# A 1024 x 1024 output projection by seven half-size products instead of eight plain tiles, with the projection before it reordered by row pairs

## Chip, cores and metric

The kernel runs on one core of a Trainium2 chip. The metric is the time of one execution on the device in microseconds. TensorE (PE; its weight loads PEld) multiplies matrices into PSUM, VectorE (DVE), ScalarE (ACT) and GpSimd (POOL) do elementwise work, SyncE (SP) mostly issues DMAs; ACT and POOL issue some too.

## The reference

One layer of a hybrid streaming encoder over 512 prompt frames and 64 sample frames (576 columns in all), in float32:

```python
def layer(x, lp, st):
    h = x + 0.5 * swiglu(rmsnorm(x, lp['norm_ffn1']), lp['w_ffn1_in'], lp['w_ffn1_out'])
    mix, new_st = mixer(rmsnorm(h, lp['norm_mix']), lp, st)
    h = h + mix
    h = h + 0.5 * swiglu(rmsnorm(h, lp['norm_ffn2']), lp['w_ffn2_in'], lp['w_ffn2_out'])
    return h, new_st
```

The mixer has three branches (a state-space scan, banded attention, a matrix memory). What matters here is its end:

```python
    g_ssd, g_att, g_ml = jnp.split(jax.nn.sigmoid(gl), 3, axis=-1)
    merged = (g_ssd * (y_ssd @ lp['w_proj_ssd']) + g_att * (y_att @ lp['w_proj_attn'])
              + g_ml * (y_ml @ lp['w_proj_mlstm']))
    return merged @ lp['w_out'], (...)
```

`w_out` and `w_proj_ssd` are 1024 x 1024, the other two 512 x 1024. A final RMSNorm follows the layer.

## The kernel before

Activations lie transposed: 1024 channels as 8 rows (tiles of 128 partitions), 576 frames along the free axis. All matmuls take float32 operands cut in two (`split`, L339 to L342): a high piece, the value rounded to the matmul's format (ScalarE cast, L340), and a low piece, the rest (VectorE subtraction, L341). A product of two operands is three matmuls: high x high, high x low, low x high.

There are two ways of multiplying.

*Plain tiles* (`gemm`, L314). The weights of 128 output channels come by two SP loads of 128 x 512 into the ring `wr` (5 buffers) and are split into the rings `ph` and `pl` (6 each). One tile covers the 576 columns in two parts (HALVES, L35), 256 and 320 wide, each a group of 8 k-steps x 3 matmuls on L281 into one of six PSUM banks taken in turn (`bank`, L200, which begins at 0 in each `wide`), and a callback empties the bank. `half_major` takes the first parts of several tiles, then their second parts; `order` turns that round.

*Seven products* (`stream`, L609, and `product`, L740). A unit is a 1024 x 256 block of weights and two output rows; weights, data and outputs are cut in 2 x 2 blocks, with 288 (FH) columns to a half, and seven products of sums and differences of blocks replace eight. Each product is 4 k-steps x 3 matmuls, 128x288, on L747. The products are called X1, A11, X3, X4, A22, A21, X2 after their weight piece. `fetch_sums` (L563) loads two blocks of a unit's weights into `x12` (ring `wx`, 4 buffers) and adds two more with an accumulating DMA from GpSimd's queue, which gives the weights of X1 and X2; `fetch` loads three single blocks into `wr`; `operand` (L591) gives the piece for one product. In the feed-forwards (`self.mixer` false) X3's weights are made in place from X1's by a GpSimd addition, and X4's from X3's by another (L594 to L598). Pieces are prepared five products ahead (AHEAD). `residual` (L778) adds one product to the residual rows in `R1` by one VectorE instruction (L786): X1 and A11 complete the second half of the first row of a pair; X3, X4, A22, A21 belong to the second row; X2 completes the first half of the first row. X1, A22, X3 and X2 of a unit accumulate in one bank, X4 and A21 in another, A11 alone. `fetch_sums` issues its load on GpSimd's queue while `self.behind` is over 0, else on SP behind a weight load of the feed-forward (`loads_after`).

The order on each engine is not that of the text: the program is laid out by a simulated timeline, which keeps dependencies, and each engine then runs its queue in that order. `high_priority` moves work ahead in it, and `issue_after(i)` places what is issued within it, on the engine of `i`, behind `i`.

The parts of the program: first feed-forward ("a", plain tiles, then a stream that ends with the four output units of its last quarter), mixer, `merge` (L1541), second feed-forward ("c": `norm`, eight plain tiles of which the first three are half-major, meanwhile the moving pieces of its stream, then the stream).

In `merge`, `half(1, ..)` and `half(2, ..)` project attention and matrix memory; the callback `put` gates a finished half tile (VectorE, L1581) and adds it into `merged` (GpSimd, L1583). The gates come from DRAM in the order of `gates` (L1557), five ahead; `self.last` is the last of these loads. Then the eight tiles of `w_proj_ssd` follow in order of rows, the last three half-major (L1626 to L1633). The residual rows are loaded back from `xs` into `R1` on GpSimd's queue behind `self.last`. Each half row of `merged` is split into `XH` and `XL`, and the eight plain tiles of `w_out` run, three half-major, two in turn, three half-major; `res` adds each half tile to `R1` (L1643). Only then `run` sets `self.behind` to 4 (L1692), so that the second feed-forward's first four `x12` loads go by GpSimd's queue, behind `self.last`.

## Time and profile before

| what | us |
|---|---|
| median of 3 runs | 1893.77 |
| lowest, highest | 1893.25, 1894.69 |
| the profiled execution | 1896.08 |
| its span, first to last instruction | 1894.4 |
| first matmul of `w_out` | 1274.44 |
| first matmul of the tile after it | 1326.53 |

The mean granted TensorE clock was 0.995 of full speed. The page gives each engine's busy time and, in 40 slices of 47 us, the tenths of a slice in which it was busy. A row of a group gives its line, engine, operation, `out<-in`, shape, count, then busy us, mean ns of one, and the engine's idle time just before, with what ended it. A row of stretches gives start:end, length, busy us and number of instructions of PE, PEld, DVE, ACT and POOL, the granted clock, the DMA share and GB/s; an instruction that crosses an edge is counted on both sides. A row of the timeline gives start, duration, engine, line, operation, and in brackets the idle time before it. A row of waits names who waited, for whom, us in total, times, and the longest. Matmuls overlap: their spacing from start to start is what counts, not their duration.

### The profile page before, as it was taken

Reading aid. Unit: us, or ns where it says so; the run is one execution under the profiler, and the core shown is the slowest. Engines: PE = TensorE matmul, PEld = TensorE weight load, DVE = VectorE, ACT = ScalarE, POOL = GpSimd, SP = SyncE. Lnnn points to the kernel's source line nnn. Section 1 sums busy time; section 2 is a strip of 40 time slices with the busy share of each in tenths; the row PEclk is TensorE's granted clock in tenths of the full one; section 3 lists DMA queues with packets and bytes.
Section 4 is the critical chain, followed back from the end, with each engine's and each line's share of the span. In section 5 each row is a group of like instructions: output and inputs, shape, how many; then the busy total and the mean of one; then the engine's idle time right before and its main releaser. Section 6 shows DMA issues by size and latency. Waiting matters only on the chain. (4 is left out here: it accounts for less than half of the span.)

```text
span 1894.4 us, 37651 instructions
## 1 busy us (share of the span) xinstructions
PE 1853.9 (98%) x13863; PEld 1807.0 (95%) x13863; DVE 1555.9 (82%) x2768; ACT 1080.1 (57%) x2438; POOL 701.4 (37%) x659
## 2 busy tenths in 40 slices
PE   9899999999999999999999999999999999999998
PEld 9899999999999879889999999999999999999998
DVE  7998998988998867767778777745899998999864
ACT  6554554655555677677666676334465554554544
POOL 3443343334231324523635453630343334333311
PEclk9999999999999999999999999999999999999999
DMA  7456556566575465755656655742446656666521
GB/s 221 110 154 167 162 153 173 157 179 173 153 203 162 116 175 159 216 156 134 188 157 185 175 163 178 238 142 77 119 118 175 165 157 164 166 163 165 152 100 57
DMA packets 130896, 299.62 MB, mean 158 GB/s; under 512 B 14464, under 2 KB 26368, under 8 KB 130712
## 3 DMA queue, kind: packets, MB, share of 16 engines
q1 hardware_dynamic: 100248, 206.24, 32.3%
q0 software_dynamic: 20848, 76.29, 21.6%
q10 hardware_dynamic: 9616, 14.69, 2.5%
q8 instruction: 109, 1.79, 0.4%
q14 instruction: 75, 0.61, 0.1%
HBM read 276.90 MB, written 20.26 MB: 157 GB/s over the span
## 5 line engine op out<-in xcount | busy, mean ns | idle before, releaser
L747 PE MATMUL acc<-TH,ph 128*128 128x288 f32 x3332 | 996.5, 300 | 21.5 <-ACT uv L655 7.9
L747 PE MATMUL acc<-TL,ph 128*128 128x288 f32 x3332 | 989.0, 297 | 0.7 <-DVE TL L341 0.7
L747 PE MATMUL acc<-TH,pl 128*128 128x288 f32 x3332 | 982.1, 296 | 2.4 <-DVE pl L341 2.4
L747 PEld LDWEIGHTS acc<-TH,ph 128*128 128x128 f32 x3332 | 626.5, 188 | 36.2 <-ACT uv L655 9.9
L747 PEld LDWEIGHTS acc<-TH,pl 128*128 128x128 f32 x3332 | 629.0, 189 | 4.7 <-DVE pl L341 3.1
L747 PEld LDWEIGHTS acc<-TL,ph 128*128 128x128 f32 x3332 | 628.5, 189 | 4.6 <-issue 3.0
L341 DVE TENSOR_TENSOR pl<-wr,ph 128x512 fp32r<-128x512 f32 x467 | 453.8, 978 | 75.3 <-ACT ph L340 64.8
L340 ACT CAST ph<-wr 128x512 fp32r<-128x512 f32 x467 | 284.9, 617 | 241.4 <-PE acc L747 134.7
L341 DVE TENSOR_TENSOR pl<-wx,ph 128x512 fp32r<-128x512 f32 x406 | 330.2, 817 | 40.7 <-ACT ph L340 34.9
L340 ACT CAST ph<-wx 128x512 fp32r<-128x512 f32 x406 | 246.7, 619 | 200.1 <-POOL wx L594 122.9
L594 POOL TENSOR_TENSOR wx<-wx,wr 128x512 f32<-128x512 f32 x168 | 258.8, 1540 | 205.5 <-DVE pl L341 163.1
L582 POOL DMA_DIRECT2D wx<-in_sblk x119 | 104.9, 914 | 504.0 <-DVE pl L341 232.4
L281 PE MATMUL acc<-YH,ph 128*128 128x320 f32 (+1 forms) x640 | 188.5, 297 | 1.4 <-ACT ph L340 0.8
L281 PE MATMUL acc<-YL,ph 128*128 128x320 f32 (+1 forms) x640 | 189.0, 296 | 0.1
L281 PE MATMUL acc<-YH,pl 128*128 128x320 f32 (+1 forms) x640 | 188.5, 295 | 0.0
L281 PEld LDWEIGHTS acc<-YH,ph 128*128 128x128 f32 x640 | 120.3, 189 | 2.4 <-ACT ph L340 1.2
L281 PEld LDWEIGHTS acc<-YL,ph 128*128 128x128 f32 x640 | 120.8, 189 | 0.6 <-DVE YL L398 0.5
L281 PEld LDWEIGHTS acc<-YH,pl 128*128 128x128 f32 x640 | 120.7, 189 | 0.0
L594 POOL TENSOR_TENSOR wy<-wx,wr 128x512 f32<-128x512 f32 x35 | 63.2, 1805 | 113.7 <-DVE pl L341 101.8
L786 DVE SCALAR_TENSOR_TENSOR R<-acc,R 128x288 f32<-128x288 f32 x196 | 87.8, 450 | 16.3 <-PE acc L747 15.2
L340 ACT CAST TH<-g 128x288 fp32r<-128x288 f32 x140 | 59.6, 432 | 55.8 <-POOL g L772 31.5
L341 DVE TENSOR_TENSOR pl<-wy,ph 128x512 fp32r<-128x512 f32 x70 | 57.1, 822 | 26.6 <-ACT ph L340 25.7
(331 smaller groups left out, 2351.3 us busy)
## 6 DMA issues: line engine op xcount, KB each, us to landing
wr<-in_sblk SPq DMA_DIRECT2D x357, 256.0 KB, 3.6
wx<-in_sblk POOLq DMA_DIRECT2D x123, 512.0 KB, 6.4
wx<-in_sblk SPq DMA_DIRECT2D x115, 512.0 KB, 3.7
wr<-in_wblk SPq DMA_DIRECT2D x110, 256.0 KB, 3.0
R<-scr_rows ACTq DMA_DIRECT2D x12, 576.0 KB, 6.1
gs<-g SPq DMA_DIRECT2D x20, 288.0 KB, 4.3
g<-gs POOLq DMA_DIRECT2D x20, 288.0 KB, 4.5
y<-ys POOLq DMA_DIRECT2D x12, 288.0 KB, 5.9
```

What stands on the lines that cost most here:

```text
L281: last = nc.tensor.matmul(ps[:, :n], wt[:, wsl], xx[:, k0 + k, a:a + n], start=(k == 0 and i == 0), stop=(k == nk - 1 and i == 2))
L340: self.cast = self.nc.scalar.copy(hi, src).ins
L341: self.nc.vector.tensor_tensor(lo, src, hi.bitcast(F32), op=ALU.subtract)
L582: nc.gpsimd.dma_start(x12, src[:, 1:3, :], accum_op=ALU.add)
L594: add = lambda o, one, two: self.nc.gpsimd.tensor_tensor(o, one, two, op=ALU.add)
L747: self.nc.tensor.matmul(ps, wt[:, wsl], xx[:, kk, :], start=(start and kk == 0 and i == 0), stop=(kk == 3 and i == 2), skip_group_check=True)
L786: self.nc.vector.scalar_tensor_tensor(o, ps, scale, o, op0=ALU.mult, op1=ALU.add)
```

## The change

`w_out` becomes four units of seven products, in the same order of products and banks as the feed-forward's stream, with `residual` in place of `res`. For it:

- `w_proj_ssd`'s tiles (and their gates) run in the order of rows 0, 4, 1, 5, 2, 6, 3, 7, which completes the pair (k, k+4) of `merged` after each two tiles. The last two, rows 3 and 7, run half-major with the second halves first.
- `operands(k)` makes the moving pieces of one pair: five subtractions and seven splits of 288 columns; it stands behind each two tiles. X1 is b22, A11 b12 - b22, X3 b11 - b22, X4 b11, A22 b22 - b21, A21 b12 - b11, X2 b21 - b11, where the first index is the row of the pair and the second the half.
- The pieces lie in buffers of the merge that have been read: those of `YH` and `YL`, four of `y`, two of the gates' ring, four of `uv`, and two new tiles.
- The first weight loads of all four units are issued by GpSimd behind the last gate load (`self.held` keeps them for the stream), the accumulating loads behind an addition into `merged`.
- The additions of weights on GpSimd are queued behind the last addition into `merged` (`adds_after`).
- `self.behind` is set in `merge`, and not again after it.

```diff
-NB = 55
-NS = 119
+NB = 47
+NS = 123
...
+class Pairs(list):
+
+    def __getitem__(self, at):
+        p, k, t = at
+        return super().__getitem__(k // 2)[p, k % 2, t]
...
+        self.held, self.adds_after = deque(), None
...
+        if self.held:
+            return self.held.popleft()
         i = len(self.splan)
...
-        add = lambda o, one, two: self.nc.gpsimd.tensor_tensor(o, one, two, op=ALU.add)
+
+        def add(o, one, two):
+            with self.tc.issue_after(self.adds_after) if self.adds_after else nullcontext():
+                self.nc.gpsimd.tensor_tensor(o, one, two, op=ALU.add)
...
-        gates = deque((8 * b + n) for b in (1, 2, 0) for n in range(8))
+        turns = (0, 4, 1, 5, 2, 6, 3, 7)
+        gates = deque((8 * b + n) for b in (1, 2, 0) for n in (range(8) if b else turns))
...
-                    nc.gpsimd.tensor_tensor(merged[:, n, sl], merged[:, n, sl], t, op=ALU.add)
+                    self.added = nc.gpsimd.tensor_tensor(merged[:, n, sl], merged[:, n, sl], t, op=ALU.add).ins
...
-        tiles = [(("w_proj_ssd", 0, 1024, n * 128, 128), [(0, put(n, 0))]) for n in range(8)]
-        self.gemm(tiles[:4], ZH, ZL)
-
+        tiles = [(("w_proj_ssd", 0, 1024, n * 128, 128), [(0, put(n, 0))]) for n in turns]
+        self.gemm(tiles[:2], ZH, ZL)
+        two = iter([self.mp.tile([128, 2, FH], F32R, name=f"W{v}{i}", tag=f"{v}{i}", bufs=1)
+                    for v in "HL" for i in range(8)])
+        pair = lambda: Pairs((next(two), next(two)))
+        late, soon = [self.xp.tile([128, 4, FH], F32R, name=f"W{i}") for i in range(2)]
+        ys = [Pairs(self.mp.tile([128, 2, FH], F32R, name="W", tag="y", bufs=4) for _ in range(2)) for _ in range(2)]
+        ops = {self.T_X1: [soon, Pairs(self.gp.tile([128, 2, FH], F32R, name="W", tag="g", bufs=BUFS["g"]) for _ in range(2))],
+               self.T_A11: [pair(), Rows(self.gp.tile([128, FH], F32R, name="uv", tag="uv", bufs=4) for _ in range(4))],
+               self.T_X3: [pair(), pair()], self.T_X4: [pair(), pair()], self.T_A22: [pair(), pair()],
+               self.T_A21: [pair(), ys[0]], self.T_X2: [ys[1], late]}
+
+        def operands(kk):
+            b11, b12, b21, b22 = (merged[:, k, h * FH:(h + 1) * FH] for k in (kk, kk + 4) for h in range(2))
+            sub = lambda o, one, two: nc.vector.tensor_tensor(o, one, two, op=ALU.subtract)
+            put = lambda src, t: self.split(src, *(v[:, kk, :] for v in ops[t]))
+            put(b22, self.T_X1)
+            for t, b in ((self.T_A11, b12), (self.T_X3, b11)):
+                d = self.xp.tile([128, FH], F32, name="d", tag="d", bufs=2)
+                sub(d, b, b22)
+                put(d, t)
+            put(b11, self.T_X4)
+            for t, one, two in ((self.T_A22, b22, b21), (self.T_A21, b12, b11), (self.T_X2, b21, b11)):
+                sub(one, one, two)
+                put(one, t)
+
+        units = [("w_out", 0, 256 * m, 256 * m + 128) for m in range(4)]
+        operands(0)
+        self.gemm(tiles[2:4], ZH, ZL)
+        self.behind = WBUFS["wx"]
+        self.held.extend([self.fetch_sums(u) for u in units])
         with tc.issue_after(self.last):
             for k in range(0, 8, 2):
                 nc.gpsimd.dma_start(self.R1[:, k:k + 2, :], self.xs[:, k:k + 2, :])
+        operands(1)
         self.gemm(tiles[4:5], ZH, ZL)
-        self.gemm(tiles[5:], ZH, ZL, half_major=True)
-        XH, XL = rows()
...
-        tiles = [(("w_out", 0, 1024, n * 128, 128), [(0, res(n))]) for n in range(8)]
-        self.gemm(tiles[:3], XH, XL, half_major=True)
-        self.gemm(tiles[3:5], XH, XL)
-        self.gemm(tiles[5:], XH, XL, half_major=True)
+        self.sums_after = self.added
+        self.gemm(tiles[5:6], ZH, ZL)
+        operands(2)
+        self.gemm(tiles[6:], ZH, ZL, half_major=True, order=(1, 0))
+        operands(3)
+        self.mixer, self.adds_after = False, self.added
+        order = ((0, self.T_X1), (1, self.T_A22), (0, self.T_A11), (1, self.T_A21), (0, self.T_X3), (1, self.T_X2),
+                 (0, self.T_X4))
+        self.stream([(u, ops, self.residual(self.R1, m, None)) for m, u in enumerate(units)], order,
+                    lambda n: {self.T_X1: n % 3, self.T_A11: 3, self.T_X4: 4 + n % 2})
+        self.adds_after = None
...
-        self.behind = WBUFS["wx"]
```

More of the change, by code (lines that the diff above doesn't have):

```diff
@@ L1631, in merge @@
                 nc.gpsimd.dma_start(self.R1[:, k:k + 2, :], self.xs[:, k:k + 2, :])
+        operands(1)
         self.gemm(tiles[4:5], ZH, ZL)
-        self.gemm(tiles[5:], ZH, ZL, half_major=True)
-        XH, XL = rows()
-        for a, n in HALVES:
-            for k in range(8):
-                sl = slice(a, a + n)
-                self.split(merged[:, k, sl], XH[:, k, sl], XL[:, k, sl])
-        def res(n):
-            def go(h, ps, sl):
-                nc.vector.scalar_tensor_tensor(self.R1[:, n, sl], ps, 0.5, self.R1[:, n, sl], op0=ALU.mult, op1=ALU.add)
-            return go
-        tiles = [(("w_out", 0, 1024, n * 128, 128), [(0, res(n))]) for n in range(8)]
-        self.gemm(tiles[:3], XH, XL, half_major=True)
-        self.gemm(tiles[3:5], XH, XL)
-        self.gemm(tiles[5:], XH, XL, half_major=True)
+        self.sums_after = self.added
[9 more added lines that the diff above has]
+        self.adds_after = None
     def run(self):
```

## The prediction

> **What bounds the kernel now.** I read the page first (busy shares and slices), then the waits of TensorE around the merge, then the busy times of the stages.
>
> ```profile
> span 1894.4 us, 37651 instructions
> PE 1853.9 (98%) x13863; PEld 1807.0 (95%) x13863; DVE 1555.9 (82%) x2768; ACT 1080.1 (57%) x2438; POOL 701.4 (37%) x659
> ...
> PE   9899999999999999999999999999999999999998
> ...
> DVE  7998998988998867767778777745899998999864
> ```
>
> TensorE is busy for 98% of the span; the merge (1170 to 1326 us) is slices 26 to 28, counted from 1, where VectorE is at 7, 4 and 5 tenths and has room. The waits of TensorE from 1170 to 1400 us, the whole merge, the norm after it and the start of the second feed-forward, are one line:
>
> ```profile
> PE acc L281 <- ACT g L662: 0.5, 1, 0.5
> ```
>
> So matmuls alone set the end here: one removed is worth its own spacing, one that waits costs what it waits. Four stretches: the end of the last projection, `w_out` as it is, one that already runs in the form the change brings (the last four output units of the first feed-forward), and the one from the second feed-forward's norm to its stream:
>
> ```profile
> core 0: us, PE busy (x) PEld busy (x) DVE busy (x) ACT busy (x) POOL busy (x), PEclk, DMA share, GB/s
> 1260.00:1274.40 14.40, 14.40 (x106) 14.40 (x105) 7.00 (x14) 4.54 (x9) 4.16 (x4) 1.00 0.22 70
> 1274.40:1326.50 52.10, 52.10 (x394) 52.10 (x393) 31.02 (x63) 23.63 (x48) 1.95 (x2) 1.00 0.24 83
> 530.40:574.90 44.50, 44.50 (x336) 44.50 (x335) 42.55 (x76) 25.85 (x49) 13.48 (x12) 1.00 0.79 214
> 1335.20:1379.20 44.00, 44.00 (x326) 43.93 (x326) 41.40 (x75) 22.11 (x43) 20.57 (x14) 1.00 0.47 114
> ```
>
> The last projection leaves VectorE half its time free, `w_out` 21 us. The 28 products of the third row (530 to 575) fill TensorE for all of 44.5 us, with VectorE at 96%: no wait, but no room either. The last row has 2.6 us left on VectorE.
>
> **The change, part by part.**
>
> Products. Before: 8 tiles x 2 halves x 8 k x 3 = 384 matmuls, half 256 wide, half 320. After: 4 units x 7 products x 4 k x 3 = 336, all 288 wide.
>
> ```profile
> 1274.44 0.28 PE L281 MATMUL acc<-YH,ph 128*128 128x256 f32 x1
> 1274.56 0.28 PE L281 MATMUL acc<-YL,ph 128*128 128x256 f32 x1
> ...
> 1300.04 0.28 PE L281 MATMUL acc<-YH,ph 128*128 128x256 f32 x1
> ```
>
> First and last are the first matmuls of output tiles 0 and 4, so four tiles, 192 matmuls, take 25.60 us: 133.3 ns each (0.12 us between those of 256 columns). The 336 of the row from 530.4 take 44.5 us, 132.4 ns, and as windows count matmuls at both edges this is the same spacing. I take 133.3 for both: 48 fewer are **-6.4 us**. The last projection keeps its 384; its new order changes no count.
>
> Added work beside TensorE. Weight pieces: 28 of 128x512 instead of 16. Moving pieces: per row pair 7 splits and 5 subtractions of 288 columns, in all 28 and 20, instead of 16 splits. Residual additions: 28 instead of 16. GpSimd additions of weights: 8, where there were none.
>
> ```profile
> L341 DVE TENSOR_TENSOR pl<-wr,ph 128x512 fp32r<-128x512 f32 x17 | 12.3, 721 | 5.2 <-ACT ph L340 4.6
> ...
> L341 DVE TENSOR_TENSOR TL<-xk,TH 128x288 fp32r<-128x288 f32 x8 | 3.6, 448 | 0.0
> ...
> L340 ACT CAST TH<-g 128x288 fp32r<-128x288 f32 x140 | 59.6, 432 | 55.8 <-POOL g L772 31.5
> ...
> L340 ACT CAST ph<-wr 128x512 fp32r<-128x512 f32 x467 | 284.9, 617 | 241.4 <-PE acc L747 134.7
> ...
> L786 DVE SCALAR_TENSOR_TENSOR R<-acc,R 128x288 f32<-128x288 f32 x29 | 13.1, 450 | 1.3 <-PE acc L747 1.0
> ...
> L594 POOL TENSOR_TENSOR wx<-wx,wr 128x512 f32<-128x512 f32 x168 | 258.8, 1540 | 205.5 <-DVE pl L341 163.1
> ```
>
> VectorE gets 12 x 0.72 + (12 + 20) x 0.45 + 12 x 0.45 = 28 us more (16 old splits put at 0.45 too); ScalarE, at 45% here, 12 x 0.62 + 12 x 0.43 = 13 us by its casts of the same shapes. Three quarters of the moving pieces are made under the last projection's tiles, where VectorE has half its time free; `w_out` itself has the mix of the row from 530.4 and, like it, the next norm behind it. I cost this at **0** in steady state, hidden by matmuls as in 530 to 575; without that cover, the 28 us less the 21 free would show as 7.
>
> The start of `w_out`. Here the analogy ends: that stream was already running. The last two tiles (rows 3 and 7) run second half first, so X1 and A11, of second halves alone, are complete 2 x 24 x 0.12 = 5.8 us before the last tile ends. The third product, X3, needs a weight sum that may only be issued behind the last addition into `merged` (`adds_after`). The old chain of one first half:
>
> ```profile
> 1258.32 0.42 DVE L1581 SCALAR_TENSOR_TENSOR g<-g,acc 128x256 f32<-128x256 f32 x1
> ...
> 1258.82 0.74 POOL L1583 TENSOR_TENSOR merged<-merged,g 128x256 f32<-128x256 f32 x1 [1.45 <-DVE g L1581]
> ```
>
> Count from the gating's start, which is about the end of the last tile's matmuls. The addition is done at 0.50 + 0.74 = 1.24; the sum for X3 (1.54) at 2.8; its cast at 3.4, its low piece at 4.1. X1 and A11 occupy TensorE until -0.16 (a matmul's 0.28 less its spacing) + 2 x 1.6 = 3.0. X3 therefore waits 0.4 for the high piece and 0.4 for the low, and ends at 5.4. The sum for X4 overwrites the buffer that X3's split has read: 4.1 + 1.54, cast and split give 6.3 and 7.0: 1.3 more. In written order this is **2.1 us**. It is 0 if the order per engine, which the program lays out itself from a simulated timeline, puts unit 1's X1 and A11 (3.2 us) ahead of X3. The bounds: 0, as at the next stream's start (in the line of waits above), and 9.1, as at the first stream's start:
>
> ```profile
> 62.60:92.00 29.40, 24.20 (x152) 22.13 (x151) 27.57 (x54) 17.86 (x42) 12.81 (x7) 0.93 0.31 90
> ```
>
> 152 matmuls need 20.3 us of those 29.4. A gain is excluded: nothing waits there now. I take **+1.4**, nearer to the chain, the only one of the three with this kernel's new wait in it. Behind the weight sum on GpSimd stand only the later sums and, later, the norm's powers.
>
> GpSimd's additions slow VectorE:
>
> ```profile
> 536.82 1.59 POOL L594 TENSOR_TENSOR wx<-wx,wr 128x512 f32<-128x512 f32 x1
> ...
> 537.36 1.61 DVE L341 TENSOR_TENSOR pl<-wx,ph 128x512 fp32r<-128x512 f32 x1
> ```
>
> The split, 0.72 otherwise, ends only after the addition does. The Trainium skill, "SBUF — State Buffer", section "Who interferes with whom", has it that a VectorE instruction with two SBUF inputs contends with a GpSimd instruction that reads SBUF, the second to issue blocked outright; the row agrees, and the rule speaks against this change, which adds eight such additions to a stage that had none. By the rule alone (8 x 0.9 us of VectorE) the time is not changed further, as the six additions in 530 to 575 are in that row's 42.55 us.
>
> The end of `w_out`. The last product completes only row 6's first half; it and row 7 finish late, so the norm's sums are later. The same junction, first feed-forward to mixer:
>
> ```profile
> 574.91 0.29 PE L747 MATMUL acc<-TH,pl 128*128 128x288 f32 x1
> 575.04 0.28 PE L281 MATMUL acc<-XH,ph 128*128 128x256 f32 x1
> ...
> 588.81 0.97 PE L390 MATMUL ps_x<-ident,sm 128*128 128x128 f32 x6
> ```
>
> No matmul is late there. One thing differs: the last unit's accumulator is `n % 3`; there n was 43, bank 1, here it is 3, bank 0, the bank that the next `gemm` takes first. If its first tile isn't put behind another, it waits for the last residual: 0.16 + 0.45, or 1.3 with a split just ahead. Between 0 and 1.3 I take **+0.3**.
>
> The second feed-forward. Its norm factors come 588.81 - 575.04 = 13.8 us after its first matmul instead of these 8.0:
>
> ```profile
> 1326.53 0.28 PE L281 MATMUL acc<-YH,ph 128*128 128x256 f32 x1
> ...
> 1334.51 0.97 PE L390 MATMUL ps_x<-ident,sm 128*128 128x128 f32 x6
> ...
> 1370.93 0.45 DVE L341 TENSOR_TENSOR TL<-xk,TH 128x288 fp32r<-128x288 f32 x1
> ...
> 1379.20 0.29 PE L747 MATMUL acc<-TH,ph 128*128 128x288 f32 x1
> ```
>
> The last low piece of X1's data is ready 7.8 us before its stream begins; 5.8 of that go, less what VectorE's 2.6 us of idle time absorb. Bounds 0 and 1.5; **+0.2**. Its first four weight sums are now loaded by SP behind a tile's weights, as in the first feed-forward, instead of on GpSimd's queue; that is over 50 us before use, hidden by the eight plain tiles: 0. The four early loads and `xs` move on GpSimd's queue behind the last gate load, a few tiles ahead of use: 0. DMA is busy at 24% in `w_out` and at 79% in the analogue without a wait: 0.
>
> Sum: -6.4 + 1.4 + 0.3 + 0.2 = **-4.5 us**. The profiled execution took 1896.1 us (span 1894.4, 1.7 around it), 2.3 above the median of the runs; on it the sum gives 1891.6. On the median, 1893.8, it gives **1889.3**.
>
> **The rivals.**
>
> All of it (R1). The products whose pieces are ready go first and X3 comes late enough: -6.4 to -5.5, about 1887.8. For it: no wait at the next stream's start and none in the row from 530.4. Against it: two chained GpSimd sums begin only after the last tile.
>
> VectorE and GpSimd pace the start (R2). In the 13 us before and 8 after the last tile's end VectorE has two row pairs' pieces (2 x 12 x 0.45 = 10.8), 5 gatings, 6 weight splits and 4 residuals (8.4), and about 5 us of blocking by some ten GpSimd additions: 24 us of work in 21. If all shows, 1.4 becomes 4 to 5, and the time 1891 to 1893.5. For it: where the streams form pieces between products they lose time too:
>
> ```profile
> 484.00:508.00 24.00, 21.16 (x137) 19.67 (x136) 24.00 (x50) 10.75 (x24) 6.85 (x7) 0.93 0.62 169
> ```
>
> 137 matmuls need 18.3 of 24 us there, VectorE full. Against it: the last row pair's later pieces are due only at the sixth to eighth product.
>
> Slower (R3): the clock. One wait of TensorE is followed by half speed:
>
> ```profile
> 90.79 0.40 PE L747 MATMUL acc<-TH,ph 128*128 128x288 f32 x1 [1.93 <-ACT P L763]
> ...
> 91.20:94.60 3.40, 3.40 (x16) 3.40 (x16) 3.11 (x6) 1.58 (x5) 1.61 (x1) 0.51 0.55 172
> ```
>
> The granted clock is 0.51 for 3.4 us: some 12 matmuls, 1.6 us, lost on top of the 1.9. If X3 and X4 each come over 2 us late (from a weight sum that ends after 5 instead of 2.75), the start costs what the first stream's start did, 9.1 with its halved stretch, and with R2's remaining 2 us: -6.4 + 11.1 + 0.5, about 1899. For it: that row's VectorE was as full. Against it: there four row pairs' pieces were late, here one. The Trainium skill, "TensorE: Matmul & The Clock Gate", section "Why this matters for your kernels", allows gaps up to about 3 us before the clock falls; this trace disagrees with 1.9. By the page a 2 us wait would cost 2, by the trace 3.6.
>
> **How the numbers follow.** Forecast, 1888.4 to 1890.8: 0.45. R1, 1887 to 1888.4: 0.22. R2, 1890.8 to 1894: 0.25. R3: 0.08. A measurement here tells about 0.2%, 3.8 us, from no change. Faster by more (below 1890.0): R1 and 0.39 of the forecast, 0.61. Within: 0.06 of the forecast, R2 and 0.02 of R3, 0.33. Slower: 0.06. The range leaves out R3, the last of R2 and a tail below R1 less the runs' spread of 0.5: 1886.9 to 1893.5.
>
> **What would show it.** 336 matmuls of 288 columns on L747 in the merge at 133 ns, and no L281 with `w_out`: the 6.4. Waits of TensorE for `ph` or `pl` in the first 8 us: the 1.4; if for the moving pieces instead, R2. A granted clock under 1 there: R3. A gap at the first matmul of the next `gemm`, ended by a residual: the 0.3. Waits at the next stream's start: the 0.2. The prediction is wrong if the last projection's tiles themselves wait, since I gave them none, or if the second feed-forward's own small waits change when the whole order is laid out anew.

## The result, and the profile after

The changed kernel takes 1911.9 us (median of 4 runs, 1911.2 to 1912.9) against 1894.2 for the kernel before on the same chip: ratio 1.0088, 95% interval 1.0076 to 1.0100. It is slower by 0.9%; forecast was 0.2% faster. The page of the changed kernel, busy shares and slices:

```profile
span 1909.4 us, 37693 instructions
PE 1854.7 (97%) x13815; PEld 1801.7 (94%) x13815; DVE 1574.2 (82%) x2824; ACT 1089.8 (57%) x2462; POOL 715.4 (37%) x671
...
PE   9899999999999999999999999999989999999998
...
PEclk9999999999999999999999999999989999999999
```

There are 48 matmuls fewer, as the products promise, yet the span is 15.0 us longer, and slice 30 (1384 to 1432 us), in the second feed-forward, now shows TensorE and its clock one tenth down. The waits of TensorE from 1170 to 1400 us, one line before (0.5 us), are these:

```profile
PE acc L761 <- ACT ph L348: 3.2, 2, 2.6
PE acc L761 <- DVE TL L349: 2.7, 3, 1.9
PE acc L761 <- ACT TH L348: 1.4, 2, 1.0
PE acc L761 <- DVE pl L349: 1.2, 2, 0.7
PE acc L289 <- DVE R L800: 0.6, 1, 0.6
```

The longest wait of all, 4.3 us, ends just behind this window, at 1400.81 us; its row stands in the account of why the prediction was wrong.

The stretches of the changed kernel (w_out from its first matmul to the tile behind it; the plain tiles of c; the start of c's stream), and the last of them in the kernel before:

```profile
1272.85:1323.10 50.25, 45.93 (x338) 44.77 (x337) 41.27 (x70) 21.58 (x39) 12.51 (x10) 1.00 0.24 80
...
1331.80:1375.80 44.00, 44.00 (x329) 43.57 (x328) 34.02 (x63) 21.21 (x42) 17.05 (x17) 1.00 0.49 121
1377.00:1405.00 28.00, 18.77 (x94) 16.68 (x93) 24.76 (x50) 15.34 (x35) 10.78 (x5) 0.82 0.25 66
```

```profile
1379.20:1407.20 28.00, 28.00 (x213) 28.00 (x212) 26.41 (x48) 19.14 (x44) 10.82 (x9) 1.00 0.43 120
```

`w_out` got shorter, 50.3 us for 52.1, though not by 6.4. In its first 28 us the second feed-forward's stream issues 94 matmuls where it issued 213, at a granted clock of 0.82. And in c's plain tiles ahead of it VectorE, which was busy for 41.4 us of 44, is busy for 34.0: it stood still where it should have made the stream's data.

To compare kernels I count the **time lost** in a stretch: of each spacing between two matmul starts what it exceeds 119, 133 or 146 ns by (256, 288 and 320 columns), for those more than 25 ns over. It holds waits and half clock alike. In us, for the start of `w_out` (1268 to 1300), its end (1300 to 1350), c's stream (1350 to 1420) and what follows (1420 to 1500); then their sum less the 0.6 of the kernel before and, where `w_out` has seven products, less 6.4; last the measured ratio:

| kernel | start | end | stream | later | gives us | ratio (95% interval) |
|---|---|---|---|---|---|---|
| before | 0 | 0.4 | 0 | 0.2 | | |
| changed | 4.8 | 1.4 | 15.9 | 0.4 | +15.5 | 1.0088 (1.0076 to 1.0100) |
| e1_swap | 5.4 | 5.8 | 2.9 | 1.6 | +8.7 | 1.0050 (1.0034 to 1.0066) |
| e2_before_late | 0 | 1.9 | 15.4 | 0.7 | +17.4 | 1.0093 (1.0070 to 1.0117) |
| e3_pool_loads | 6.6 | 1.4 | 16.9 | 0.8 | +18.7 | 1.0095 (1.0079 to 1.0111) |
| e4_no_after | 3.5 | 1.4 | 15.7 | 0.4 | +14.0 | 1.0078 (1.0062 to 1.0094) |
| f1_swap_bank | 5.9 | 3.3 | 2.9 | 1.3 | +6.4 | 1.0032 (1.0019 to 1.0045) |
| f2_order | 3.9 | 2.2 | 2.8 | 1.6 | +3.5 | 1.0018 (1.0006 to 1.0030) |
| f3_order_no_after | 5.2 | 2.2 | 3.1 | 1.8 | +5.3 | 1.0018 (1.0008 to 1.0028) |
| f4_order_prio | 5.3 | 2.2 | 3.1 | 1.8 | +5.4 | 1.0016 (1.0006 to 1.0026) |
| g1_early_sums | 3.1 | 1.4 | 16.4 | 0.8 | +14.7 | 1.0086 (1.0071 to 1.0100) |
| g2_early_residual | 1.8 | 2.2 | 3.2 | 1.7 | +1.9 | 1.0010 (1.0001 to 1.0020) |
| g3_two_na | 1.8 | 2.8 | 3.5 | 1.1 | +2.2 | 1.0014 (1.0004 to 1.0024) |
| h1_free_memory | 1.8 | 0.4 | 2.8 | 1.5 | -0.5 | 0.9998 (0.9989 to 1.0007) |
| h2_free_old_order | 4.1 | 0.4 | 2.8 | 1.6 | +1.9 | 0.9996 (0.9987 to 1.0005) |
| i1_free_two_na | 1.8 | 0.3 | 1.9 | 1.6 | -1.4 | 0.9998 (0.9989 to 1.0008) |
| i2_free_two_na_no_after | 1.1 | 0.3 | 1.9 | 1.8 | -1.9 | 0.9988 (0.9977 to 0.9998) |

The kernels go by their labels; each is described below. One us is 0.0005 of the ratio. The account from single profiles agrees with the ratios to 2.7 us or better; what lies ahead of 1268 us alone loses 53.7 to 58.7 us from one profile to another, and the start can differ by 1.4 us between two profiles of the same order of work (`f2_order` and `f4_order_prio`, below).

Why did VectorE stand still in c? The norm came late. From the timelines of the changed kernel, then of the kernel before: scaling (L405; L397 before), the first squares (L356), the square totals (L374; L366) and the factors spread over the partitions (L398; L390):

```profile
1320.78 0.62 ACT L348 CAST ph<-wr 128x512 fp32r<-128x512 f32 x1 [0.98 <-PE acc L761]
1321.31 0.51 ACT L405 ACTIVATE YH<-R,cst 128x256 fp32r<-128x256 f32 x1
1322.38 0.42 ACT L356 ACTIVATE na<-R 128x256 f32<-128x256 f32 x1 [0.57 <-PE acc L761]
...
1337.47 0.50 PE L374 MATMUL ps_x<-ones,na 128*128 128x1 f32 x4
1341.73 0.61 PE L398 MATMUL ps_x<-ident,sm 128*128 128x128 f32 x4
...
1350.85 0.97 PE L398 MATMUL ps_x<-ident,sm 128*128 128x128 f32 x6
```

```profile
1277.98 0.51 ACT L397 ACTIVATE YH<-R,cst 128x256 fp32r<-128x256 f32 x1 [0.91 <-DVE R L1643]
...
1320.07 0.50 PE L366 MATMUL ps_x<-ones,na 128*128 128x1 f32 x4
1324.33 0.61 PE L390 MATMUL ps_x<-ident,sm 128*128 128x128 f32 x4
```

c's first matmul is at 1323.12 and 1326.53. Before, the first scaling started 48.6 us ahead of it and the first totals stood 6.5 us ahead; now the first of all 16 scalings starts 1.8 us ahead, the accumulator `na` 0.7 us, behind the last product, and the first totals come 14.4 us later than c's first matmul. The second factors come 27.7 us behind it instead of 8.0. The last residuals of rows 0 to 3 had been added 16 us before that first scaling, those of rows 4 and 5 some 5 us before it.

By the addresses in the built program, `na` of the new norm (188640 to 189920 of each partition) overlaps the new tile `W0` (184416 to 189024), which the very last product, X2 of the last unit, reads; its square buffers and `YH` and `YL` overlap `W1`, the temporaries `d`, the gates' ring and `uv`, where X1's and A11's pieces lie. Before, none of this memory was read by `w_out`. That gives the **memory theory**: the norm waits for memory. Against it stand the **order theory** (rows 6 and 7 are finished last, so the norm must be late), the **loads theory** (c's first weight loads, moved from GpSimd's queue to SP's), and for the start of `w_out` the chain of GpSimd's sums against VectorE's pace.

### The profile page after: what moved, and what is told of

The parts are those of the page before. It is cut to its first block, busy times and chain, and to the rows that moved or that the text cites. A ratio compares the mean times of both kernels' runs of the same rounds, so it can differ in the third digit from the quotient of the medians.

```text
span 1909.4 us, 37693 instructions
## 1 busy us (share of the span) xinstructions
PE 1854.7 (97%) x13815; PEld 1801.7 (94%) x13815; DVE 1574.2 (82%) x2824; ACT 1089.8 (57%) x2462; POOL 715.4 (37%) x671
## 5 line engine op out<-in xcount | busy, mean ns | idle before, releaser
L349 DVE TENSOR_TENSOR pl<-wx,ph 128x512 fp32r<-128x512 f32 x422 | 343.1, 816 | 47.5 <-ACT ph L348 41.5
L607 POOL TENSOR_TENSOR wx<-wx,wr 128x512 f32<-128x512 f32 x176 | 274.2, 1558 | 221.6 <-DVE pl L349 182.6
L289 PE MATMUL acc<-YL,ph 128*128 128x320 f32 (+1 forms) x512 | 150.4, 296 | 0.5 <-DVE YL L406 0.5
L289 PE MATMUL acc<-YH,ph 128*128 128x320 f32 (+1 forms) x512 | 148.7, 298 | 2.0 <-DVE R L800 0.6
L289 PE MATMUL acc<-YH,pl 128*128 128x320 f32 (+1 forms) x512 | 149.7, 296 | 0.0
L800 DVE SCALAR_TENSOR_TENSOR R<-acc,R 128x288 f32<-128x288 f32 x224 | 100.3, 450 | 21.6 <-PE acc L761 20.6
L289 PEld LDWEIGHTS acc<-YH,ph 128*128 128x128 f32 x512 | 95.2, 188 | 3.5 <-ACT YH L405 1.0
L289 PEld LDWEIGHTS acc<-YL,ph 128*128 128x128 f32 x512 | 96.4, 188 | 0.9 <-DVE YL L406 0.9
L289 PEld LDWEIGHTS acc<-YH,pl 128*128 128x128 f32 x512 | 96.1, 188 | 0.1
L786 POOL TENSOR_TENSOR g<-g,P 128x288 f32<-128x288 f32 x56 | 63.7, 1137 | 45.3 <-ACT P L785 45.3
```

The costliest lines, as they stand in the source:

```text
L289: last = nc.tensor.matmul(ps[:, :n], wt[:, wsl], xx[:, k0 + k, a:a + n], start=(k == 0 and i == 0), stop=(k == nk - 1 and i == 2))
L349: self.nc.vector.tensor_tensor(lo, src, hi.bitcast(F32), op=ALU.subtract)
L607: self.nc.gpsimd.tensor_tensor(o, one, two, op=ALU.add)
L786: nc.gpsimd.tensor_tensor(s["g"][:, 1, :], s["g"][:, 1, :], a, op=ALU.mult)
L800: self.nc.vector.scalar_tensor_tensor(o, ps, scale, o, op0=ALU.mult, op1=ALU.add)
```

## The experiments

### The norm's memory

**The kernel before, with the overlap alone.** No product, order or load is touched:

```diff
         XH, XL = rows()
+        XH[7] = self.xp.tile([128, 5 * T], F32R, name="big")
```

> The kernel before, where row 7's high piece for w_out lies in a tile five times as large as it needs, at 184416 to 195936 of each partition, so that the next norm's na, sq and YH overlap a tile which w_out's last tile reads. Nothing else is changed, and w_out keeps its eight plain tiles. Memory theory: the norm bunches behind w_out here too, the totals of the first half come some 12 to 15 us after c's first matmul instead of 6.6 before it, and c's stream starts with waits: 1905 to 1912 against 1893.8. Order theory and loads theory: within 2 us of before, as neither the order of the rows nor the loads are touched.

Measured: 1912.6 us against 1896.1. The first totals are 13.8 us behind c's first matmul by the timeline, and by the stretches c's stream starts as in the changed kernel:

```profile
1324.12 0.62 PE L281 MATMUL acc<-YH,ph 128*128 128x256 f32 x3 [0.97 <-ACT YH L397]
...
1337.92 0.50 PE L366 MATMUL ps_x<-ones,na 128*128 128x1 f32 x4
```

```profile
1376.50:1406.00 29.50, 21.05 (x108) 18.02 (x107) 26.31 (x51) 15.93 (x36) 12.05 (x6) 0.83 0.25 63
```

So the overlap alone makes a loss of the same size at c's stream, 15.4 us for 15.9, with plain tiles in the old order of rows and the old loads.

**The changed kernel, with two buffers exchanged.**

```diff
-               self.T_A11: [pair(), Rows(self.gp.tile([128, FH], F32R, name="uv", tag="uv", bufs=4) for _ in range(4))],
+               self.T_A11: [late, Rows(self.gp.tile([128, FH], F32R, name="uv", tag="uv", bufs=4) for _ in range(4))],
...
-               self.T_A21: [pair(), ys[0]], self.T_X2: [ys[1], late]}
+               self.T_A21: [pair(), ys[0]], self.T_X2: [ys[1], pair()]}
```

> The changed kernel with two buffers exchanged: A11's high pieces lie in the tile W0 and X2's low pieces in two pairs of the old YH and YL, so that the buffer which the second feed-forward's square accumulator na overlaps is read last by the last unit's A11 and no longer by its X2, the very last product. Memory theory (the norm of the second feed-forward waits because its tiles lie where the last products' pieces lie): its first scaling starts 6 to 9 us before the last product ends instead of 1.8 us before c's first matmul, the totals of the first half come within 6 us of c's first matmul instead of 14.2, the second factors near 15 instead of 27.7, the waits at the start of c's stream shrink from 12 us to under 3 and the half clock there goes; time 1895 to 1900 (changed kernel 1911.9). Order theory (the norm is late because rows 6 and 7 are finished last): the factors move by under 3 us, time 1909 to 1913. Loads theory (the first sums' loads of c on SP's queue are what is late): no change, 1910 to 1913.

Measured: 1.0050. The scaling starts 14.4 us ahead of c's first matmul, the second factors come 18.1 us behind it (27.7 before the exchange; the memory theory said near 15), and the stream loses 2.9 us for 15.9. The order of rows, unchanged here, can hold no more than that. The forecast of 1895 to 1900 was missed all the same (1904.9), as the end of `w_out` lost 4.4 us more. Timeline and stretch there:

```profile
1313.78 0.51 ACT L405 ACTIVATE YH<-R,cst 128x256 fp32r<-128x256 f32 x1
...
1328.22 0.36 PE L289 MATMUL acc<-YH,ph 128*128 128x256 f32 x1 [2.63 <-DVE R L800]
```

```profile
1328.20:1332.60 4.40, 4.38 (x24) 4.40 (x25) 2.47 (x6) 2.43 (x6) 0.00 (x0) 0.62 0.84 247
```

The norm's work, crowded into these 14 us, and the splits of c's first weights stand ahead of the last residual on VectorE; bank 0 comes free 2.6 us late, and a clock of 0.62 follows. `YH` itself overlaps nothing that the last four products read, neither here nor in the changed kernel, and yet its first scaling starts close to the last read of `W0` in both: 0.6 us into the last product that reads it in the changed kernel, 0.6 us behind that product here. Why it comes no sooner stays open. That the pool of the new tiles comes free only as one piece isn't the reason: in `h1_free_memory` (below) the first scaling starts at 1287.65, and `na`, which overlaps the last of that pool's new tiles to be read, waits until 1298.17.

**The loads** of c's first sums back on GpSimd's queue:

```diff
+        self.behind = WBUFS["wx"]
         with self.ffn_phase("c"):
```

> The changed kernel with self.behind set again before the second feed-forward, so that its first four x12 loads go by GpSimd's queue behind the last gate load, as before. Loads theory: the waits at the start of c's stream go, 1896 to 1900. Memory theory and order theory: within 2 us of 1911.9, the totals of the first half still 14 us behind c's first matmul.

Measured: 1.0095, totals still 14.3 us behind; the loads theory falls.

### The start of w_out

The weight sums free of the last addition:

```diff
-        self.mixer, self.adds_after = False, self.added
+        self.mixer, self.adds_after = False, None
```

> The changed kernel without adds_after: the weight sums on GpSimd needn't be queued behind the last addition into merged. Chain theory of w_out's start (X3 waits since its sum may only follow the last addition): X3's sum is done before X1 and A11 end, the 5 us lost at the start fall to 1 to 3, and the time to 1908 to 1910. Pace theory (VectorE's row pair 3 and its late gating set the start): the sum is early and X3 then waits for its moving pieces instead, under 1.5 us gained, 1910.5 to 1912. The 16 us at c's stream are untouched by either.

Without `adds_after` the start lost 3.5 us for 4.8: the long wait for X3's cast (2.6 us) is gone, and waits for a residual, for moving pieces and for low pieces stand in its place. The gain of 1.3 us is what the pace theory allows (under 1.5), and less than the chain theory asks. Why is VectorE in arrears? ScalarE's queue ahead of the last tiles in the changed kernel, by the timeline, and VectorE's waits from 1260 to 1275 us:

```profile
1257.72 0.43 ACT L348 CAST WH<-merged 128x288 fp32r<-128x288 f32 x1 [2.04 <-POOL merged L1598]
1263.23 0.62 ACT L348 CAST ph<-wx 128x512 fp32r<-128x512 f32 x1 [5.08 <-DMA wx<-in_sblk]
```

```profile
DVE pl L349 <- ACT ph L348: 3.1, 1, 3.1
```

The cast of X1's weights waits 5.1 us for the accumulating load (issued at 1257.63), the casts of row pair 2 stand behind it on ScalarE, and VectorE idles 3.1 us shortly before it is wanted most. One line moved:

```diff
+        self.sums_after = self.added
         operands(1)
         self.gemm(tiles[4:5], ZH, ZL)
-        self.sums_after = self.added
```

> The changed kernel with one line moved: the accumulating loads of w_out's first sums follow the last addition of the tile before (sums_after set ahead of tiles[4:5] instead of behind it), one tile of 6.4 us sooner. In the changed kernel ScalarE's cast of the first X1 weights stood 5.1 us for such a load (issued at 1257.63, landed 5.5 us on), the casts of row pair 2 stood behind it, and VectorE idled 3.1 us, 10 to 13 us before the last tile's end. Transfer theory of w_out's start: with the load there in time VectorE makes pair 2's pieces 3 to 5 us sooner, is not in arrears at the last tile, and the 4.8 us lost from 1268 to 1300 fall to 1 to 2.5; time 1908 to 1910 (changed kernel 1911.9), as c's stream still waits. Chain theory (X3's sum behind the last addition): a wait of 2.75 us in front of X3 stays, within 1 us of the changed kernel.

Measured: the start loses 3.1 us for 4.8 (longest wait 1.4 us for 2.6), between the two forecasts; the total stays at 1.0086, and the gain of 1.7 us in the trace is inside that interval. By this pair of profiles the loads, which the prediction didn't cost, were a third of the loss there.

Three runs had the exchange, the other bank (below) and a new order of products, which puts 4.8 us of products instead of 3.2 ahead of the first X3:

```diff
-        order = ((0, self.T_X1), (1, self.T_A22), (0, self.T_A11), (1, self.T_A21), (0, self.T_X3), (1, self.T_X2),
-                 (0, self.T_X4))
+        order = ((0, self.T_X1), (1, self.T_X3), (0, self.T_A11), (1, self.T_X4), (1, self.T_A22), (1, self.T_A21),
+                 (1, self.T_X2))
```

> The kernel with the exchange and the other bank, and the seven products in another order: X1, X3 of the unit before, A11, X4, A22, A21, X2 of the unit before; so X1 of units 0 and 1 and A11 of unit 0 stand ahead of the first X3, 4.8 us instead of 3.2, and the last unit's A11 is read 9 products before the end instead of 7. Chain theory of the start: X3's weights come 4.3 us after X1 and A11 (wait 2.75 plus 0.8, then the half clock); 1.6 us more cover takes the wait below 1.9 us and the half clock goes: the 4.8 to 6.6 us lost from 1268 to 1300 fall to 1 to 3, time 1895.5 to 1898. Pace theory: VectorE has the same work in the same time, so other waits take its place, 4 us or more still lost there, time 1898 to 1901.

The same with the edit of `e4_no_after`:

> As the run with the new order, without adds_after. Chain theory: the first X3's sum is off the path, the start loses under 1.5 us, 1894 to 1896.5. Pace theory: within 1 us of the run with the new order.

The same with `adds_after` kept, and the gatings moved ahead:

```diff
-                nc.vector.scalar_tensor_tensor(o, t, 1.0, ps, op0=ALU.add, op1=ALU.mult)
+                with tc.high_priority(offset=EVAC if branch == 0 else 0):
+                    nc.vector.scalar_tensor_tensor(o, t, 1.0, ps, op0=ALU.add, op1=ALU.mult)
```

> As the run with the new order (adds_after kept), with the gatings of the last projection moved ahead on VectorE's queue (high_priority 300): the last gating ran at 1274.82 us, 1.8 us after its tile's last matmul, behind splits of the row pair. Queue theory: it then starts within 0.3 us of it, the last addition, X3's sum and its pieces come 1.5 us sooner, and 1 to 2 us of the start go: 1894 to 1896.5. Pace theory: the splits pushed back are late instead, no change against the new order.

Measured: 3.9, 5.2 and 5.3 us lost at the start. The third run doesn't test the queue theory: on every engine its instructions run in the same order as in `f2_order`, so the priority moved no gating (the last one starts 2.7 us behind its tile's last matmul, 2.5 in `f2_order`). It is a second profile of the same order instead. Its waits at the start are the same to 0.2 us (1.86 and 1.26 us; 1.65, 1.26 and 0.20 in `f2_order`), and the 1.4 us more are a halved clock behind them; so 1.9 us, below which the chain theory saw the half clock go, is no bound. Stretches of `f4_order_prio` and `f2_order`:

```profile
1283.00:1286.40 3.40, 3.40 (x15) 3.18 (x14) 3.32 (x6) 2.70 (x5) 0.24 (x1) 0.51 0.25 82
```

```profile
1283.40:1286.80 3.40, 3.20 (x24) 2.97 (x23) 3.40 (x7) 3.16 (x6) 0.20 (x1) 1.00 0.25 82
```

Dropping `adds_after` gained nothing. In the run without `adds_after` a gating of the last tile ran 6.3 us behind that tile's last matmul, with VectorE busy for 12.23 of 13 us (stretch, then timeline):

```profile
1269.10:1282.10 13.00, 9.88 (x77) 9.36 (x75) 12.23 (x23) 6.09 (x13) 6.66 (x6) 1.00 0.28 72
```

```profile
1273.31 0.28 PE L289 MATMUL acc<-ZH,pl 128*128 128x256 f32 x1
...
1279.62 0.41 DVE L1596 SCALAR_TENSOR_TENSOR g<-g,acc 128x256 f32<-128x256 f32 x1
```

So with late loads the start is paced by VectorE; whether an earlier gating would have helped, no run tells. With the loads a tile sooner (`g2_early_residual`, next section) the same order loses 1.8 us; and with the loads sooner but the old order 4.1 (`h2_free_old_order`). By these profiles both were needed; the times of `h1_free_memory` and `h2_free_old_order` don't show a difference.

### The end of w_out

The run with the exchange, with another bank for X1:

```diff
-                    lambda n: {self.T_X1: n % 3, self.T_A11: 3, self.T_X4: 4 + n % 2})
+                    lambda n: {self.T_X1: (n + 1) % 3, self.T_A11: 3, self.T_X4: 4 + n % 2})
```

> The run with the two buffers exchanged (1904.9), and X1 of unit n in bank (n + 1) % 3 instead of n % 3, so that the last unit's accumulator is bank 1 and not bank 0, which the next tile takes first. In the run with the exchange alone TensorE waited 2.8 us there for the last residual, with the half clock behind it. Bank theory: the wait at c's first matmul goes, 4 to 5.5 us of lost spacing between 1300 and 1345 us with it, time 1899 to 1901. Rival (VectorE's queue is in arrears there with the norm's work, and the next tile or its evacuation waits anyway): 1903 to 1905.

The wait at c's first matmul went as the bank theory says; 2.5 us of the 5.8 went, since the next waits were for other residuals and for the norm's pieces, which is the rival's part. Then, on `f2_order`, the early loads and the residuals ahead of the norm's work (`self.evac` is 2000 in `merge`, else EVAC):

```diff
-            with nullcontext() if self.mixer else self.tc.high_priority(offset=EVAC):
+            with nullcontext() if self.mixer else self.tc.high_priority(offset=self.evac):
```

> The kernel with the exchange, the other bank and the new order of products (ratio 1.0018 to before), with the accumulating loads a tile sooner and the residual additions of w_out ahead of the next norm's work on VectorE (high_priority 2000 instead of 300; the norm has 1500). Transfer theory: of the 3.9 us lost at the start 2 to 3 go. Priority: of the 2.2 us lost from 1300 to 1350 (products waiting 1.34 and 0.63 us for residuals) 1.5 to 2 go. Left are 2.8 + 1.6 us at c's stream: ratio 0.9995 to 1.0005. If both theories fall, 1.0018 stays.

The start did as forecast (3.9 to 1.8), the end did not move (2.2): priority alone doesn't mend it.

### The norm's memory set free wholly

The pieces of row pair 3 now go into the rows of `merged` that the earlier pairs have done with, and the `xp` tiles hold only X1's first pieces. The gates' ring and `uv` are used no more:

```diff
-        merged = self.mp.tile([128, 8, T], F32, name="merged")
+        merged = Rows(self.mp.tile([128, T], F32, name="merged", tag=f"M{i}", bufs=1) for i in range(8))
...
+        soon = [self.xp.tile([128, 2, FH], F32R, name=f"W{i}") for i in range(2)]
+        two, dead, ops, tiles4 = chain(soon, two, ys), iter((0, 4, 1, 5, 2, 6)), {}, {}
+        for t in (self.T_X1, self.T_A11, self.T_X3, self.T_X4, self.T_A22, self.T_A21, self.T_X2):
+            tiles4[t] = next(two), next(two), next(two), next(two) if t == self.T_X2 else next(dead)
+            ops[t] = [Rows((v[:, 0, :], v[:, 1, :], tiles4[t][2][:, h, :], None)) for h, v in enumerate(tiles4[t][:2])]
...
+                if isinstance(m, int):
+                    m = self.mp.tile([128, 2, FH], F32R, name="W", tag=f"M{m}", bufs=1)
+                for h in range(2):
+                    list.__setitem__(ops[t][h], 3, m[:, h, :])
```

> The run with the early residual (new order of products, other bank, early accumulating loads; ratio 1.001), with all pieces that are read late laid outside the memory of the next norm: row pair 3's pieces lie in the rows of merged that pairs 0 to 2 have done with, and the two new tiles of xp hold only X1's pieces of pairs 0 and 1, last read 11 products before the end; nothing lies in the gates' ring and uv any more. The norm's scaling can then begin some 29 us before the end of w_out instead of 11, as in the kernel before (23). Memory theory: what is still lost behind w_out (2.2 us at its end and 3.2 + 1.7 us at c's stream) comes from the norm's work bunched into the last 11 us; it falls to 0.5 and to 1 to 2.5, ratio 0.9975 to 0.9995. Full-VectorE theory (the rest is VectorE's added work, wherever the norm's is put): 1.0005 to 1.0015 as before.

Measured: 0.9998, between the two forecasts. The first scaling and the first square:

```profile
1287.65 0.51 ACT L406 ACTIVATE YH<-R,cst 128x256 fp32r<-128x256 f32 x1 [2.06 <-DVE R L801]
...
1298.17 0.42 ACT L357 ACTIVATE na<-R 128x256 f32<-128x256 f32 x1 [1.72 <-PE acc L762]
```

Scaling starts 31.9 us ahead of c's first matmul (1319.52), and the end of `w_out` loses what it lost before the change, 0.4 us. That is still later than in the kernel before: there the first scaling is 48.6 us ahead, not the 23 that the expectation names. The stream still loses 2.8 + 1.5, so the memory theory got the end right and the stream only in part. The same with the old order of products:

> As the run before it with the changed kernel's own order of products (and its residuals at priority 300). Cover theory: X3 stands 1.6 us less far from the start, 1 to 2 us more lost there, ratio 0.0005 to 0.001 above the run before it. If the order of products makes no difference once the accumulating loads come early, both are within 0.0005 of each other.

In the trace it loses 2.3 us more at the start, in the times nothing (0.9996); the profile's part ahead of the merge happened to lose 2.7 us less, so single profiles don't decide this one.

What holds the stream back still? With memory free, the second factors are at 1337.08, 17.6 us behind c's first matmul instead of 8.0:

```profile
1324.43 0.50 PE L375 MATMUL ps_x<-ones,na 128*128 128x1 f32 x4
...
1332.52 0.71 PE L375 MATMUL ps_x<-ones,na 128*128 128x1 f32 x6
1337.08 0.97 PE L399 MATMUL ps_x<-ident,sm 128*128 128x128 f32 x6
```

The single `na` makes the second half's squares wait for the first totals. Two of them: on `g2_early_residual`, where the norm is free in part; on `h1_free_memory`; and on that without `adds_after`:

```diff
-            self.hidden_tiles(name)
+            self.hidden_tiles(name, na=2 if name == "c" else 1)
```

> As the run before it, with two accumulators na for the second feed-forward's norm instead of one, so that the second half's squares needn't wait for the totals of the first. The second totals come some 3 us sooner than 13 us after c's first matmul. If the 2.8 + 1.6 us lost at c's stream come from the late factors, 1 to 3 us of them go: ratio 0.998 to 0.9995. If they come from VectorE being full in that stage, nothing changes.

> The kernel with the norm's memory wholly free (ratio 0.9998), with two accumulators na for that norm. There the second factors still come 17.4 us behind c's first matmul, 9.5 later than in the kernel before, VectorE is then full from 20 us behind it until 80, and 2.8 + 1.5 us are lost at c's stream. Late-factor theory: the second totals come 3 to 4 us sooner, the factors at 13.4 to 14.5, and 1 to 3 of the 4.3 us go: ratio 0.998 to 0.9993. Full-VectorE theory: VectorE gains the idle time but the stream's waits for evacuations stay within 0.7 us: 0.9995 to 1.0002.

> As the run before it without adds_after, so that the first X3's sum may stand ahead of the last additions into merged. 1.8 us are left at the start, in waits for X3's low piece (1.33) and one more (0.5). Chain theory: 1 us of it goes, ratio 0.0005 lower. Pace theory: no change, or the gatings behind the sum come later and it is 0.0005 higher.

With the norm still bunched two accumulators brought the second factors 4.1 us sooner (13.4 us behind) and gained nothing (1.0014 for 1.0010). With memory free the second factors come 3.4 us sooner (14.2 us behind) and the stream loses 0.9 us less, just under what the late-factor theory gave; the ratio (0.9998) lies in the range of the full-VectorE theory. So late factors are not shown to be the cause. Without `adds_after` the start loses 1.1 us for 1.8, as the chain theory says, once VectorE is no longer in arrears. That version is the fastest: 1893.4 us against 1896.1, ratio 0.9988 (0.9977 to 0.9998). The interval ends just short of 1 and overlaps that of the run before it, and it is the best of fifteen versions with seven products, so a gain of a tenth of a per cent is likely at most. All waits of TensorE over 0.2 us that are left in it from 1170 to 1400 us:

```profile
PE acc L762 <- DVE g L775: 0.5, 1, 0.5
PE acc L762 <- DVE pl L350: 0.5, 1, 0.5
PE acc L762 <- DVE P L781: 0.3, 1, 0.3
```

The 3.7 us that c's stream and what follows still lose there (before: 0.2) go with six waits of 0.2 to 0.5 us for evacuations, four by VectorE and two by ScalarE. VectorE has no pause in the 10 us ahead of the first, at 1380 us, but is busy for 8.2 us of the 10 ahead of the second and 6.7 ahead of the fourth, so a full VectorE doesn't explain them all. What does, and what part the second factors have, which remain 6 us later than in the kernel before, no run here tells.

## Why the prediction was wrong

**The step that failed** is the one on the second feed-forward: "Its norm factors come 588.81 - 575.04 = 13.8 us after its first matmul instead of these 8.0", of which 7.8 us of slack would swallow most, +0.2. In the changed kernel the first factors came 18.6 us and the second, which the 13.8 meant, 27.7 us behind, and the +0.2 was 15.9. The analogy with the first feed-forward's end was of order alone; there the next norm's tiles lie in other memory. That the pieces lie in buffers of the merge "that have been read", and in two new tiles, was on record ahead of the prediction; who takes that memory next was not asked. The run of the kernel before with the overlap alone loses 15.4 us there, and the run with all of it taken away loses 0.4 at the end and 2.8 at the stream. No rival had this: the slowest ended near 1899 us, by the clock.

The step would have been wrong without the overlap too, though by less. In `i2_free_two_na_no_after` the factors come 14.2 us behind, nearly as foreseen, and the stream alone loses 1.9 us, over the bound of 1.5; the slack didn't swallow it, and why is open.

**How lateness becomes 16 us.** The stream's data is made by VectorE from the factors on; started 20 us later, it ran into the stream. The longest wait shows a third party, GpSimd, which adds X3's weights there. Timeline and stretch of the changed kernel, and the group of the same additions in its `w_out`:

```profile
1394.04 6.07 POOL L607 TENSOR_TENSOR wx<-wx,wr 128x512 f32<-128x512 f32 x1 [11.69 <-DVE pl L349]
1394.48 0.45 DVE L349 TENSOR_TENSOR TL<-xd,TH 128x288 fp32r<-128x288 f32 x1
...
1398.17 0.81 DVE L349 TENSOR_TENSOR TL<-g,TH 128x288 fp32r<-128x288 f32 x2
...
1400.81 0.61 PE L761 MATMUL acc<-TH,ph 128*128 128x288 f32 x1 [4.34 <-ACT ph L348]
```

```profile
1400.80:1404.20 3.40, 3.39 (x14) 3.39 (x15) 2.20 (x4) 2.70 (x8) 0.96 (x2) 0.52 0.81 136
```

```profile
L607 POOL TENSOR_TENSOR wx<-wx,wr 128x512 f32<-128x512 f32 x8 | 11.2, 1401 | 20.2 <-DVE pl L349 20.2
```

An addition of 1.4 us took 6.07, the first 4.95 of them beside a VectorE without a pause; TensorE waited 4.34 us for what is made from it, and then ran at 0.52 of its clock for 3.4 us.

**The start of w_out**, +1.4, was 4.8: the mechanism (X3's sum behind the last addition) was one part, with a wait of 2.6 us for the 0.8 of the text's chain; the other was the accumulating loads. The text gave 0 to "the four early loads and `xs`", "a few tiles ahead of use", and didn't cost these at all: they were issued 15.2 us ahead of `w_out`, but ScalarE came to the first cast that needs them 14.7 us ahead of it and waited 5.1. The rival that VectorE and GpSimd pace the start (4 to 5 us) had the size right, and the runs without `adds_after` bear it out.

**The end of w_out**, +0.3, was 1.0, at the place named (bank 0, the last residual) and within its bounds of 0 to 1.3. **The products**, -6.4, were right: the 50.25 us of the new `w_out` are 336 spacings of 133.3 ns (44.8 us) and 5.6 us lost, and with the losses accounted the ratios of all seven-product kernels follow within 2.7 us. **The steady state** at 0 was right too: from 1284 to 1321 us no matmul of the changed kernel waits. **c's loads by SP** cost nothing, as said. The rival by the clock had a mechanism that did occur in the changed kernel, but behind the waits at c's stream, not in `w_out`.

## What to carry to other kernels

When a change puts its data into memory that "has been read", ask what the next stage lays over it: a tile that is read last delays whoever is allocated there next, and a norm that should run beside the last matmuls then runs behind them. Put what is read last where the next stage has nothing, and what is read first where it starts. A junction that looks the same elsewhere in the kernel proves nothing unless its buffers were free too.

## What the runs showed of the hardware

The clock doesn't follow the length of a wait alone. The same wait, before the first X3, in the run with the exchange (timeline, stretch) and in the changed kernel (the same):

```profile
1280.09 0.40 PE L761 MATMUL acc<-WH,ph 128*128 128x288 f32 x1 [2.50 <-ACT ph L348]
```

```profile
1280.09:1284.87 4.78, 4.05 (x16) 3.47 (x17) 2.51 (x7) 2.49 (x6) 1.42 (x1) 0.64 0.00 0
```

```profile
1278.77 0.53 PE L761 MATMUL acc<-WH,ph 128*128 128x288 f32 x2 [2.58 <-ACT ph L348]
```

```profile
1278.77:1283.00 4.23, 3.11 (x17) 2.42 (x18) 2.86 (x7) 1.93 (x5) 1.43 (x1) 1.00 0.00 0
```

After 2.50 us the granted clock was 0.64, after 2.58 us it stayed at 1.00; and in `f4_order_prio` it fell to 0.51 behind two waits of 1.86 and 1.26 us, where in `f2_order` it stayed at 1.00 behind 1.65 and 1.26, with the same order of work. What decides it, no run here tells.

And GpSimd can be kept waiting for far longer than one VectorE instruction: 6.07 us (above) for an addition of 1.40 on the mean, while a dozen VectorE subtractions of 0.45 us ran back to back; 6.07 again in `e2_before_late`, and 4.47 once in the kernel before, at 84.47 us. It is not the rule: of the changed kernel's 19 other such additions that lay wholly beside three or more VectorE instructions back to back, 17 took 1.4 to 1.8 us. The Trainium skill, "SBUF — State Buffer", section "Who interferes with whom", has the first to issue hold the shared ports for the whole of its instruction and the other blocked; the trace agrees that GpSimd is held up, and shows that it can be for many instructions on end; that it is the shared access and nothing else is inferred from the two running side by side.
